# Three FFN pairs kept in PSUM through norm and convolution, the second norm's scaled input in PSUM, one square on ScalarE, and the last eight adaLN blocks later

## The chip, the core and the metric

The kernel runs on one core of a Trainium2 chip. Five engines work on their own instruction streams, each in the order in which its stream was written: TensorE (PE in the profile, its weight loads as PEld), VectorE (DVE), ScalarE (ACT), GpSimd (POOL) and SyncE (SP), which here issues the transfers. They wait for each other by semaphores. The metric is the device time of one execution in microseconds (us); lower is better.

## The reference, cut to what matters

One decoder layer on 256 tokens of width 1024 in float32. The part that the change touches is the end of the layer:

```
mod = c @ w_ada + b_ada                       # 6 x 1024 adaLN numbers
sh_m, sc_m, gt_m, sh_f, sc_f, gt_f = split(mod, 6)
h = rms_norm(x, norm_mix) * (1 + sc_m) + sh_m
...                                           # attention and delta net, mixed
x = x + gt_m * (mixed @ w_out)
h = rms_norm(x, norm_ffn) * (1 + sc_f) + sh_f
u = causal_depthwise_conv(h @ ffn_up, ffn_conv) + ffn_conv_b      # width 3
u_gate, u_val = split(u, 2)
x = x + gt_f * ((silu(u_gate) * u_val) @ ffn_down)
return rms_norm(x, norm_final)
```

FFN_DIM is 2816, that is 22 blocks of 128 channels for the gate and 22 for the value.

## The kernel before

Activations lie transposed: channels on the 128 partitions, the 256 tokens along the free axis, so that the width of 1024 is eight tiles (k = 0 to 7). Every matrix product is made from two parts of each operand: a rounded high part and the rest, the low part. For an activation these are `fh` and `fl` (`hh`/`hl`, `gh`/`gl`, `ah`/`al` elsewhere), for a weight `whi` and `wlo` (`dhi`/`dlo` for the down matrix), and one block of a product is three matmuls: high by high, low by high, high by low. `split` (L232) makes the two parts of a weight piece of 128x1024 that `rawload` (L227) has fetched: ScalarE casts the high part (L241), and GpSimd or VectorE subtracts it (L242), three pieces of eight on GpSimd at this stage. Five raw buffers turn for all such pieces, five for `whi`, four for `wlo`; the adaLN blocks use the same raw buffers (`wada`, L206 to L218: one transfer of 512 KB and one VectorE reduction, L212).

Before the FFN, the output projection (`lin` on `mxh`, L1059) gives the new residual `x1` and the sum of squares in PSUM (`ss2`). So that TensorE need not wait for the norm, the first three FFN pairs (NU = 3; a pair is the gate block and the value block of the same 128 channels) are multiplied with the un-normed input `gh`/`gl` into six PSUM banks, `up` (L1074 to L1085), with the shift as an extra column. Then `rsqrt` (L198) gives `r`; the six banks are scaled by `r` (L1092), get their shift as a bias (L1093) and are further called `u`. The normed input itself, `mt` (L1098), `fh` (L1099) and `fl` (L1100), is made for pairs 3 to 21.

For each pair f in the FFN loop (L1131): `lin` multiplies (L264, L266, L267), `fconv` (L1105) makes the three convolution taps, one on ScalarE (L1108) and two on VectorE (L1110), for the gate (`ug`) and the value (`uv`); then the gate's silu (L1144), the product with the value (L1147) and its two parts `ah` (L250) and `al` (L251). From pair 5 on, the down projection of pair f-5 follows (L1126 to L1128, into the four banks `dn`), and in pairs 4 to 11 one adaLN block of `gt_f` (L1154). The last eight pairs' down matmuls come at the end (L1163), with the residual and the last norm.

Tile's scheduler decides the order of the instructions on each engine when the kernel is built, from its own estimate of durations, and gives each PSUM tile one of eight banks. A bank is handed on as a whole: who writes the next tile into it waits for the last reader of the one before.

Of the kernel before, what the change touches and what calls it, by code (L numbers as in the profile page):

```python
# [15 lines left out]
AF = mybir.ActivationFunctionType  # L16
ALU = mybir.AluOpType
# [4 lines left out]
P = 128  # L22
D = 1024
KB = D // P
T = 256
# [8 lines left out]
NU = 3  # L34
# [9 lines left out]
PARTS = 2  # L44
OUTS = {0: 0, 1: 1, 3: 2, 5: 4, 7: 6}
QG = 1
ADA = ([0] * 4, [1] * 8, [1] * 8, 2, 4)
WARM = (2, 4)
GC = math.sqrt(2.0 / math.pi)

# [51 lines left out]
def build(tc, a, probe=None):  # L102
    nc = tc.nc
    V, S, G, TE = nc.vector, nc.scalar, nc.gpsimd, nc.tensor
    with ExitStack() as ctx:
# [8 lines left out]
        def bank(name, tag, shape=(P, 512)):  # L114
            return ps.tile(list(shape), F32, name=name, tag=tag, bufs=PB[tag])
# [7 lines left out]
        def tl(name, tag, shape=None, dt=F32):  # L123
            n, w = TAGS[tag]
            return wk.tile(list(shape or (P, w)), dt, name=name, tag=tag, bufs=n)
# [45 lines left out]
        def preload(src):  # L171

            S.activation(kcon[:, 1:2], src, AF.Abs_reciprocal_sqrt)
# [15 lines left out]
            cs = slice(512 * i, 512 * i + 512)  # L189
            TE.matmul(flat(kob[5 + i]), ones[:1], crow[:, cs], start=True, stop=True)  # L190

        def newton(y, v, t, n=1.0):

            V.tensor_tensor(t, y, y, op=ALU.mult)
            V.scalar_tensor_tensor(t, t, -0.5 / n, v, op0=ALU.mult, op1=ALU.mult)
            V.scalar_tensor_tensor(y, t, 1.5, y, op0=ALU.add, op1=ALU.mult)

        def rsqrt(v):  # L198

            r, t = tl("r", "mz"), tl("nt", "tc")  # L200
            S.activation(r, v, AF.Abs_reciprocal_sqrt, scale=1.0 / D)
            newton(r, v, t, D)
            return r


# [8 lines left out]
        def ada(n=1):  # L214

            for _ in range(n):
                m = next(mods)
                adasum(m, adaload(m))  # L218
# [34 lines left out]
        def lin(src, hh, hl, blocks=2, tag="lin"):  # L253

            parts = loadw(src)
            o = bank("lin", tag, (P, blocks, T))
            n = KB // len(parts)
            parts = [[v.rearrange("p (k c) -> p k c", k=n) for v in p] for p in parts]
            for i, (hi, lo) in enumerate(parts):
                for b in range(blocks):  # L260
                    cs = slice(b * P, b * P + P)
                    for j in range(n):
                        k = i * n + j
                        TE.matmul(o[:, b], hi[:, j, cs], hh[k], start=k == 0 and b == 0, stop=False,  # L264
                                  skip_group_check=True)
                        TE.matmul(o[:, b], hi[:, j, cs], hl[k], start=False, stop=False, skip_group_check=True)  # L266
                        TE.matmul(o[:, b], lo[:, j, cs], hh[k], start=False,  # L267
                                  stop=k == KB - 1 and b == blocks - 1, skip_group_check=True)
            return o
# [24 lines left out]
        def scaled(k):  # L294
            t = tl("mt", "tc")
            V.scalar_tensor_tensor(t, x[k], acol[:, k:k + 1], r, op0=ALU.mult, op1=ALU.mult)
            return t
# [34 lines left out]
        ac(0)  # L332
        adasum(1, wada[1])
        r = rsqrt(ssq[:, :T])
        t = scaled(0)
        shifted(0, t, V)
# [97 lines left out]
        w = wp.tile([P, D], F32, name="wraw", tag="wraw", bufs=NRAW)  # L434
        nc.sync.dma_start(out=w[:, :512], in_=a["wg"])
        w = w[:, :512].rearrange("p (k c) -> p k c", k=KB)
# [100 lines left out]
        for h in range(NH):  # L537
            for c in range(2):
                eq = bank("eq", "gd")
                u = 8 * c + h  # L540
# [12 lines left out]
                            op=ALU.add, negate=True)  # L553
# [35 lines left out]
        for p in range(4):  # L589
            o = lin(a["win"][p], hh, hl)  # L590
# [18 lines left out]
        n = range(2)  # L609
# [62 lines left out]
        def delta(p):  # L672
# [52 lines left out]
            for _ in range(3):  # L725
                newton(y_, v_, t_)
# [17 lines left out]
        def gates_z(p):  # L744
            o = lin(a["win"][14 + p], hh, hl)
            ada(ADA[0][p])
            for b in range(2):
# [243 lines left out]
        mg = [[tl(f"mg{m}{b}", "mz") for b in range(8)] for m in range(2)]  # L991
        for m in range(2):
            for p in range(4):
                o = lin(a["win"][18 + 4 * m + p], hh, hl)
                for b in range(2):
                    S.activation(mg[m][2 * p + b], o[:, b], AF.Tanh, scale=0.5)
                ada(ADA[1][4 * m + p])

# [13 lines left out]
        for p in range(4):  # L1012
            for m, (w, yh, yl) in enumerate((("pn", yah, yal), ("pg", ybh, ybl))):
                o = lin(a[w][p], yh, yl)
                ada(ADA[2][2 * p + m])
                for b in range(2):
                    t = mg[m][2 * p + b]
# [40 lines left out]
        for p in range(4):  # L1058
            o = lin(a["wo"][p], mxh, mxl)  # L1059
            ada(ADA[3])  # L1060
            residual(o, p, x1, x, gm, ss2, 4, True)
# [12 lines left out]
        ups = [[bank("up", "up" if f < 2 else "lin") for b in range(2)] for f in range(NU)]  # L1074
        for i in range(2):
            up = [[v.rearrange("p (k c) -> p k c", k=4) for v in loadw(a["up"][f][i:i + 1])[0]] for f in range(NU)]
            for j in range(4):
                k = 4 * i + j
# [7 lines left out]
        r = rsqrt(ss2[:, :T])  # L1086
        wsh = small(NU, 2)
        for f in range(NU):
            for b in range(2):
                o, u = ups[f][b], tl("u", "mg")  # L1090
                V.tensor_copy(wsh[:, f, b:b + 1], o[:, T:T + 1])
                V.tensor_tensor(u, o[:, :T], r, op=ALU.mult)  # L1092
                S.activation(u, u, AF.Identity, bias=wsh[:, f, b:b + 1])  # L1093
                ups[f][b] = u
        fh, fl = big("fh"), big("fl")
        for k in range(KB):
            t = tl("mt", "tc")
            V.scalar_tensor_tensor(t, x1[k], acol[:, 8 + k:9 + k], r, op0=ALU.mult, op1=ALU.mult)  # L1098
            S.activation(fh[k], t, AF.Identity, bias=shf[:, k:k + 1])  # L1099
            V.scalar_tensor_tensor(fl[k], t, shf[:, k:k + 1], fh[k].bitcast(F32), op0=ALU.add, op1=ALU.subtract)  # L1100
# [4 lines left out]
        def fconv(src, blk, name):  # L1105
            acc = tl(name, "mg")
            w0 = COLS["fconv"][0] + 3 * blk
            S.activation(acc, src, AF.Identity, bias=cl("fconvb", blk), scale=col[:, w0 + 2:w0 + 3])  # L1108
            for sft in (1, 2):
                V.scalar_tensor_tensor(acc[:, sft:], src[:, :T - sft], col[:, w0 + 2 - sft:w0 + 3 - sft],  # L1110
                                       acc[:, sft:], op0=ALU.mult, op1=ALU.add)
            return acc
# [18 lines left out]
        for f in range(NF):  # L1131
            if f < NU:
                o = ups[f]
            else:
                o = lin(a["up"][f], fh, fl, tag="lin" if f % 2 else "gd")
                o = [o[:, b] for b in range(2)]
            ug = fconv(o[0], f, "ug")
            uv = fconv(o[1], NF + f, "uv")

            if f >= NU:  # L1140
                t, w = o
            else:
                t, w = tl("ft", "mg"), uv
            S.activation(t, ug, AF.Silu)  # L1144
            if f == NF - 1:
                preload(t[:, :1])
            V.tensor_tensor(w, t, uv, op=ALU.mult)  # L1147
            uv = w
            acts[f] = tl("ah", "mg", dt=F32R), tl("al", "mg", dt=F32R)
            split_act(*acts[f], uv)  # L1150
            if LAG <= f < NF - TAIL:
                down(f - LAG, parts_of(f - LAG))
            if ADA[4] <= f < ADA[4] + 8:
                ada()  # L1154
# [19 lines left out]
        r = rsqrt(ss3[:, :T])  # L1174
# [70 lines left out]
```

## Time and profile before

| | |
|---|---|
| three runs | 658.63, 657.24, 657.26 us; median 657.26 |
| profiled execution | 658.84 us, of which the span from first to last instruction 657.0 us |
| busy | PE 592.5 us (90%), DVE 524.3 (80%), ACT 382.8 (58%), POOL 341.2 (52%) |
| mean granted TensorE clock | 0.954 |
| chain that ended last | PE 42%, DVE 33%, DMA 11%, issue 6%, ACT 6% |

The profile is one execution. "Idle before" an instruction is the time in which its engine stood still, with the instruction that released it behind the arrow. Busy time of an engine includes the time that an instruction, once begun, takes longer than usual. A matmul's own duration (0.28 us) overlaps the next one's, so the pace is read from counts in a stretch. The granted clock of 1.00 is 2.4 GHz, 0.50 is 1.2 GHz.

### The profile page before, as it was taken

The page shows a single profiled execution, that of the slowest core. Times are in us where ns is not written, and L with a number is a line of the kernel's source. Part 1 is how long each engine was busy: PE and PEld are TensorE (multiplying, and loading weights), DVE is VectorE, ACT ScalarE, POOL GpSimd, SP SyncE. Part 2 cuts the span into 40 slices and gives each one's busy share as a digit, 9 for nine tenths or more (in the row PEclk, how much of TensorE's full clock was granted, in tenths as well). Part 3 has the DMA queues.
Part 4 walks back from the last instruction along what each step waited for, and adds up shares of the span by engine and source line. Part 5 has one row for each costly group of instructions (what it writes and reads, how often), then busy time and mean ns, then how long its engine had stood idle before and what let it go on. Part 6 is the DMA issues. An engine that isn't in the chain of part 4 may idle for free.

```text
span 657.0 us, 13696 instructions
## 1 busy us (share of the span) xinstructions
PE 592.5 (90%) x5128; PEld 559.5 (85%) x5128; DVE 524.3 (80%) x1209; ACT 382.8 (58%) x855; POOL 341.2 (52%) x239
## 2 busy tenths in 40 slices
PE   7998997999989998999898998798967989999994
PEld 4987997988979886999777997797966979999994
DVE  5999869789998998788967779769996676675745
ACT  4335988645555676687775532565554456655443
POOL 3324996825584876475521443455552258544431
PEclk9899999899997989999999999699896989999998
DMA  7779555334784734233304557754556546553501
GB/s 287 280 278 336 217 197 193 122 129 136 228 280 169 252 131 161 66 129 130 130 33 162 175 185 256 265 210 156 193 198 252 198 166 218 193 193 129 193 1 64
DMA packets 35365, 119.73 MB, mean 182 GB/s; under 512 B 4962, under 2 KB 5730, under 8 KB 35299
## 3 DMA queue, kind: packets, MB, share of 16 engines
q1 hardware_dynamic: 35298, 118.86, 51.4%
q8 instruction: 40, 0.66, 0.4%
q14 instruction: 27, 0.21, 0.1%
HBM read 117.66 MB, written 1.18 MB: 181 GB/s over the span
## 4 chain that ended last, share of the span: by engine, by line
PE 42%; DVE 33%; DMA 11%; issue 6%; ACT 6%; SPq 1%; DVEq 0%; ACTq 0%
DMA wada<-in_ada 9%; PE lin L266 9%; PE lin L267 8%; PE lin L264 8%; DVE wada L212 7%; DVE wlo L242 4%; PE dn L1127 2%; PE dn L1128 2%; PE dn L1126 2%; DVE pp L920 2%; ACT whi L241 1%; PE y L966 1%; DVE uv L1110 1%; DVE pp L904 1%; DVE cacc L396 1%
## 5 line engine op out<-in xcount | busy, mean ns | idle before, releaser
L242 POOL TENSOR_TENSOR wlo<-wraw,whi 128x1024 fp32r<-128x1024 f32 x90 | 230.2, 2567 | 180.2 <-ACT whi L241 95.7
L241 ACT CAST whi<-wraw 128x1024 fp32r<-128x1024 f32 x144 | 150.2, 1048 | 86.1 <-PE lin L266 26.7
L264 PE MATMUL lin<-hh,whi 128*128 128x256 f32 x384 | 111.8, 291 | 1.1 <-DVE cacc L396 0.7
L267 PE MATMUL lin<-hh,wlo 128*128 128x256 f32 x384 | 111.3, 291 | 0.0
L266 PE MATMUL lin<-hl,whi 128*128 128x256 f32 x384 | 111.2, 290 | 0.0
L212 DVE CUSTOM_DVE_ANT_0 wada<-wada,cb,col 128x1024 f32<-128x1024 f32 x48 | 85.5, 1783 | 18.4 <-DMA wada<-in_ada 18.1
L266 PE MATMUL lin<-fl,whi 128*128 128x256 f32 x304 | 87.5, 289 | 2.9 <-DVE fl L1100 2.9
L264 PE MATMUL lin<-fh,whi 128*128 128x256 f32 x304 | 87.2, 288 | 0.2
L267 PE MATMUL lin<-fh,wlo 128*128 128x256 f32 x304 | 86.9, 287 | 0.0
L242 DVE TENSOR_TENSOR wlo<-wraw,whi 128x1024 fp32r<-128x1024 f32 x54 | 82.0, 1519 | 5.2 <-ACT whi L241 2.2
L264 PEld LDWEIGHTS lin<-hh,whi 128*128 128x128 f32 x384 | 74.9, 195 | 2.0 <-ACT whi L241 0.9
L267 PEld LDWEIGHTS lin<-hh,wlo 128*128 128x128 f32 x384 | 75.1, 196 | 0.6 <-issue 0.2
L266 PEld LDWEIGHTS lin<-hl,whi 128*128 128x128 f32 x384 | 75.0, 195 | 0.6
L266 PEld LDWEIGHTS lin<-fl,whi 128*128 128x128 f32 x304 | 60.3, 198 | 3.3 <-DVE fl L1100 3.3
L1126 PE MATMUL dn<-ah,dhi 128*128 128x256 f32 x176 | 49.0, 288 | 13.1 <-ACT ah L250 13.1
L264 PEld LDWEIGHTS lin<-fh,whi 128*128 128x128 f32 x304 | 60.1, 198 | 0.6 <-ACT whi L241 0.3
L267 PEld LDWEIGHTS lin<-fh,wlo 128*128 128x128 f32 x304 | 60.2, 198 | 0.0
L242 POOL TENSOR_TENSOR dlo<-wraw,dhi 128x1024 fp32r<-128x1024 f32 x14 | 34.9, 2498 | 44.0 <-ACT dhi L241 41.7
L1127 PE MATMUL dn<-al,dhi 128*128 128x256 f32 x176 | 49.3, 283 | 0.3 <-DVE al L251 0.2
L1128 PE MATMUL dn<-ah,dlo 128*128 128x256 f32 x176 | 49.0, 281 | 0.0
L1126 PEld LDWEIGHTS dn<-ah,dhi 128*128 128x128 f32 x176 | 33.6, 196 | 14.1 <-ACT ah L250 14.1
L913 ACT ACTIVATE pp<-pp,misc 128x128 f32<-128x128 f32 x64 | 28.4, 446 | 13.8 <-DVE misc L905 13.7
(410 smaller groups left out, 1620.3 us busy)
## 6 DMA issues: line engine op xcount, KB each, us to landing
wraw<-in_win SPq DMA_DIRECT2D x52, 512.0 KB, 3.7
wada<-in_ada SPq DMA_DIRECT2D x48, 512.0 KB, 4.5
wraw<-in_up SPq DMA_DIRECT2D x44, 512.0 KB, 3.8
wraw<-in_down SPq DMA_DIRECT2D x22, 512.0 KB, 3.7
wraw<-in_wko SPq DMA_DIRECT2D x16, 512.0 KB, 5.2
wraw<-in_pn SPq DMA_DIRECT2D x8, 512.0 KB, 3.5
wraw<-in_pg SPq DMA_DIRECT2D x8, 512.0 KB, 3.6
wraw<-in_wo SPq DMA_DIRECT2D x8, 512.0 KB, 4.0
```

What stands on the lines that cost most here:

```text
L212: V.tensor_tensor_reduce(w, w, cb, 1.0, cl("bada", m), ALU.mult, ALU.add, mod[:, m:m + 1])
L241: recent[S] = S.copy(hi, w).ins
L242: recent[e] = e.tensor_tensor(lo, w, hi.bitcast(F32), op=ALU.subtract).ins
L264: TE.matmul(o[:, b], hi[:, j, cs], hh[k], start=k == 0 and b == 0, stop=False, skip_group_check=True)
L266: TE.matmul(o[:, b], hi[:, j, cs], hl[k], start=False, stop=False, skip_group_check=True)
L267: TE.matmul(o[:, b], lo[:, j, cs], hh[k], start=False, stop=k == KB - 1 and b == blocks - 1, skip_group_check=True)
L396: V.scalar_tensor_tensor(acc[:, sft:], src[:, :T - sft], col[:, w0 + 3 - sft:w0 + 4 - sft], acc[:, sft:], op0=ALU.mult, op1=ALU.add)
L913: S.activation(pv, pv, AF.Exp, bias=mx[:, 1 + w, t, r:r + 1], accum_out=sm[:, 1 + w, t, r:r + 1])
L920: (G if 2 * w + t in POOLP else V).tensor_scalar(pv, pv, wt[:, 1 + w, t, r:r + 1], None, op0=ALU.mult)
L1126: TE.matmul(o, hi[:, cs], ah, start=f == 0 and b % 2 == 0, stop=False, skip_group_check=True)
L1127: TE.matmul(o, hi[:, cs], al, start=False, stop=False, skip_group_check=True)
L1128: TE.matmul(o, lo[:, cs], ah, start=False, stop=f == NF - 1 and b % 2 == 1, skip_group_check=True)
```

## The change

Four edits. ADA's last number moves the eight adaLN blocks of the FFN loop from pairs 4 to 11 to pairs 12 to 19. `rsqrt` squares its first estimate on ScalarE and not on VectorE, in all three norms (the first, the second and the last one). The six banks of the first three pairs are scaled, shifted, convolved and multiplied in place, where they were copied to SBUF by the scaling. And `mt` of the second norm lies in PSUM, two k in one bank.

```diff
-ADA = ([0] * 4, [1] * 8, [1] * 8, 2, 4)
+ADA = ([0] * 4, [1] * 8, [1] * 8, 2, 12)
...
-        def newton(y, v, t, n=1.0):
-
-            V.tensor_tensor(t, y, y, op=ALU.mult)
+        def newton(y, v, t, n=1.0, squared=False):
+
+            if not squared:
+                V.tensor_tensor(t, y, y, op=ALU.mult)
...
             S.activation(r, v, AF.Abs_reciprocal_sqrt, scale=1.0 / D)
-            newton(r, v, t, D)
+            S.activation(t, r, AF.Square)
+            newton(r, v, t, D, True)
...
-                o, u = ups[f][b], tl("u", "mg")
+                o, u = ups[f][b], ups[f][b][:, :T]
...
-            t = tl("mt", "tc")
+            if k % 2 == 0:
+                mt = bank("mt", "at", (P, 2, T))
+            t = mt[:, k % 2]
...
-            if f >= NU:
-                t, w = o
-            else:
-                t, w = tl("ft", "mg"), uv
+            t, w = o
```

The banks as the built programs have them around the second norm, in order of use:

```
bank  before                          changed
0     up (pair 2 gate), lin 5          up (pair 2 gate), lin 5
1     up (pair 2 value), dn            up (pair 2 value), dn
2     up (pair 0 gate), lin 4          up (pair 0 gate), lin 3, dn
3     up (pair 0 value), dn            up (pair 0 value), lin 4
4     up (pair 1 gate), dn             up (pair 1 gate), dn
5     lin (wo), lin 3                  lin (wo), mt k0 k1, mt k4 k5, dn
6     up (pair 1 value), dn            up (pair 1 value), lin 6
7     ss2, lin 6                       ss2, mt k2 k3, mt k6 k7
```

The order of the instructions, first on TensorE at the beginning of pair 3 (`lin_6343` before, `lin_6330` now; the numbers name buffers, a wait names the engine whose semaphore is waited for). Before:

```order
L264 MATMUL lin_6343<-fh_6234,whi_6333 128x256 [waits Activation_49]
L266 MATMUL lin_6343<-fl_6242,whi_6333 128x256 [waits DVE_49]
L267 MATMUL lin_6343<-fh_6234,wlo_6334 128x256 [waits Pool_49]
L264 MATMUL lin_6343<-fh_6235,whi_6333 128x256 [waits Activation_49]
L266 MATMUL lin_6343<-fl_6243,whi_6333 128x256 [waits DVE_49]
L267 MATMUL lin_6343<-fh_6235,wlo_6334 128x256
```

Now, at the same place, right behind the last `up` matmul:

```order
L266 MATMUL lin_6330<-fh_6228,whi_6320 128x256 [waits DVE_49,PE_49,Activation_49]
L268 MATMUL lin_6330<-fl_6236,whi_6320 128x256
L269 MATMUL lin_6330<-fh_6228,wlo_6321 128x256 [waits Pool_49]
L266 MATMUL lin_6330<-fh_6229,whi_6320 128x256 [waits Activation_49]
L268 MATMUL lin_6330<-fl_6237,whi_6320 128x256
L269 MATMUL lin_6330<-fh_6229,wlo_6321 128x256
```

The matmuls are the same; the first one's wait for VectorE is now for the first pair's product, `up_6019<-up_6018,uv_6280`, the last reader of bank 2. In the same way pair 4's first matmul waits for `al_6287` (bank 3), pair 5's for `up_6023<-up_6022,uv_6308` (bank 0), and the first down matmul for the third pair's `al` (bank 1). Down blocks stand one pair of up matmuls or so later than before: the block of pair f-5 behind pair f.

On VectorE, from the second norm on, before:

```order
L194 TENSOR_TENSOR nt_6205<-r_6204 128x256
L195 SCALAR_TENSOR_TENSOR nt_6205<-nt_6205,ss2_5692 128x256
L196 SCALAR_TENSOR_TENSOR r_6204<-nt_6205,r_6204 128x256
L1098 SCALAR_TENSOR_TENSOR mt_6250<-x10_5681,misc_69,r_6204 128x256
L1098 SCALAR_TENSOR_TENSOR mt_6254<-x11_5682,misc_69,r_6204 128x256
L1098 SCALAR_TENSOR_TENSOR mt_6258<-x12_5683,misc_69,r_6204 128x256
```

and now:

```order
L196 SCALAR_TENSOR_TENSOR nt_6205<-nt_6205,ss2_5692 128x256
L197 SCALAR_TENSOR_TENSOR r_6204<-nt_6205,r_6204 128x256
L1093 COPY misc_69<-up_6018 128x1
L1102 SCALAR_TENSOR_TENSOR mt_6244<-x10_5681,misc_69,r_6204 128x256
L1102 SCALAR_TENSOR_TENSOR mt_6251<-x12_5683,misc_69,r_6204 128x256
L1094 TENSOR_TENSOR up_6018<-up_6018,r_6204 128x256
L1104 SCALAR_TENSOR_TENSOR fl_6236<-mt_6244,misc_69,fh_6228 128x256
L1102 SCALAR_TENSOR_TENSOR mt_6244<-x11_5682,misc_69,r_6204 128x256
L1114 SCALAR_TENSOR_TENSOR ug_6276<-up_6018,col_80,ug_6276 128x255
L1104 SCALAR_TENSOR_TENSOR fl_6237<-mt_6244,misc_69,fh_6229 128x256
L1114 SCALAR_TENSOR_TENSOR ug_6276<-up_6018,col_80,ug_6276 128x254
L1104 SCALAR_TENSOR_TENSOR fl_6238<-mt_6251,misc_69,fh_6230 128x256
```

Before, all eight `mt` stood ahead of the first copy out of `up_6018`; now that copy stands ahead of the first `mt`, and `mt`, `fl` and the first pair's work are mixed.

Further on, on VectorE, the first pair's product and what stands around it, before:

```order
L1110 SCALAR_TENSOR_TENSOR uv_6290<-u_6214,col_80,uv_6290 128x255
L1110 SCALAR_TENSOR_TENSOR ug_6286<-u_6210,col_80,ug_6286 128x254
L242 TENSOR_TENSOR dlo_6562<-wraw_6559,dhi_6561 128x1024
L1110 SCALAR_TENSOR_TENSOR uv_6290<-u_6214,col_80,uv_6290 128x254
L212 ISA wada_6595,misc_69<-wada_6595,cb_95,col_80 128x1024
L212 ISA misc_69 128x1
L1147 TENSOR_TENSOR uv_6290<-ft_6294,uv_6290 128x256
L251 TENSOR_TENSOR al_6298<-uv_6290,ah_6297 128x256
```

and now:

```order
L1114 SCALAR_TENSOR_TENSOR uv_6280<-up_6019,col_80,uv_6280 128x255
L1114 SCALAR_TENSOR_TENSOR uv_6280<-up_6019,col_80,uv_6280 128x254
L1148 TENSOR_TENSOR up_6019<-up_6018,uv_6280 128x256
L244 TENSOR_TENSOR dlo_6546<-wraw_6543,dhi_6545 128x1024
L1104 SCALAR_TENSOR_TENSOR fl_6241<-mt_6258,misc_69,fh_6233 128x256
L1104 SCALAR_TENSOR_TENSOR fl_6242<-mt_6265,misc_69,fh_6234 128x256
L253 TENSOR_TENSOR al_6287<-up_6019,ah_6286 128x256
L1102 SCALAR_TENSOR_TENSOR mt_6265<-x17_5688,misc_69,r_6204 128x256
```

The product stands before the last `mt` and the last three `fl` now, 30 instructions from the copy out of `up_6018` (itself counted); no adaLN reduction (`wada`) stands between. In the changed program the eight reductions lie between the `al` of pair 7 and the `al` of pair 15, and the loads of these blocks on SP likewise behind the weights of pair 11.

## Rows read from the trace of the kernel before

**Rows 1.** The page's slices: 40 equal parts of the span, tenths.

```profile
PE   7998997999989998999898998798967989999994
```

**Rows 2.** Windows: PE, PEld, DVE, ACT, POOL busy (x instructions), clock, DMA share, GB/s.

```profile
452.00:476.00 24.00, 21.01 (x151) 20.31 (x149) 24.00 (x34) 13.29 (x20) 14.66 (x5) 0.86 0.47 167
476.00:540.00 64.00, 50.53 (x371) 48.93 (x370) 47.95 (x65) 31.31 (x49) 26.10 (x11) 0.87 0.58 209
540.00:640.00 100.00, 100.00 (x879) 100.00 (x878) 62.46 (x98) 56.85 (x90) 50.72 (x20) 1.00 0.43 153
502.50:508.00 5.50, 5.50 (x26) 5.50 (x27) 4.82 (x6) 1.41 (x2) 2.08 (x1) 0.50 0.42 144
```

**Rows 3.** Waits of PE from 452 to 540: us in total, times, longest.

```profile
PE dn L1126 <- ACT ah L250: 13.1, 5, 4.9
PE lin L266 <- DVE fl L1100: 2.9, 2, 2.5
```

**Rows 4.** Timeline of PE: start us, us, instruction, [idle before <- releaser].

```profile
450.70 0.28 PE L1085 MATMUL up<-gl,whi 128*128 128x258 f32 x1
...
452.63 0.28 PE L264 MATMUL lin<-fh,whi 128*128 128x256 f32 x1
...
493.38 0.79 PE L1126 MATMUL dn<-ah,dhi 128*128 128x256 f32 x2 [4.89 <-ACT ah L250]
...
502.45 1.23 PE L1126 MATMUL dn<-ah,dhi 128*128 128x256 f32 x4 [3.58 <-ACT ah L250]
```

**Rows 5.** Timeline of DVE, second norm and first pairs.

```profile
445.65 2.61 DVE L194 TENSOR_TENSOR nt<-r 128x256 f32<-128x256 f32 x1
...
449.22 3.26 DVE L1098 SCALAR_TENSOR_TENSOR mt<-x,misc,r 128x256 f32<-128x256 f32 x8
...
455.18 5.49 DVE L1100 SCALAR_TENSOR_TENSOR fl<-mt,misc,fh 128x256 fp32r<-128x256 f32 x3
...
462.12 0.47 DVE L1100 SCALAR_TENSOR_TENSOR fl<-mt,misc,fh 128x256 fp32r<-128x256 f32 x1
...
462.92 0.14 DVE L1091 COPY misc<-up 128x1 f32<-128x1 f32 x1
462.98 0.41 DVE L1092 TENSOR_TENSOR u<-up,r 128x256 f32<-128x256 f32 x1
...
467.95 2.61 DVE L1110 SCALAR_TENSOR_TENSOR uv<-u,col,uv 128x254 f32<-128x254 f32 x1
...
473.83 2.60 DVE L1147 TENSOR_TENSOR uv<-ft,uv 128x256 f32<-128x256 f32 x1
...
501.20 0.43 DVE L1147 TENSOR_TENSOR lin<-lin,uv 128x256 f32<-128x256 f32 x1 [0.51 <-ACT lin L1144]
...
507.18 1.21 DVE L242 TENSOR_TENSOR wlo<-wraw,whi 128x1024 fp32r<-128x1024 f32 x1
```

**Rows 6.** Timeline of POOL in the same stretch.

```profile
442.25 5.73 POOL L242 TENSOR_TENSOR wlo<-wraw,whi 128x1024 fp32r<-128x1024 f32 x2 [1.89 <-PE up L1085]
...
454.89 5.10 POOL L242 TENSOR_TENSOR wlo<-wraw,whi 128x1024 fp32r<-128x1024 f32 x2 [6.91 <-ACT whi L241]
```

**Rows 7.** Timeline of ACT at the second norm.

```profile
444.44 1.04 ACT L241 CAST whi<-wraw 128x1024 fp32r<-128x1024 f32 x1
...
449.74 2.51 ACT L1099 ACTIVATE fh<-mt,misc 128x256 fp32r<-128x256 f32 x6 [4.26 <-DVE mt L1098]
```

**Rows 8.** Groups of DVE from 476 to 540: busy, mean ns, idle before, releaser.

```profile
L212 DVE CUSTOM_DVE_ANT_0 wada<-wada,cb,col 128x1024 f32<-128x1024 f32 x6 | 11.9, 1977 | 5.4 <-DMA wada<-in_ada 5.4
```

**Rows 9.** Timeline of DVE: first and last `al` of 14 after 540.

```profile
547.92 0.42 DVE L251 TENSOR_TENSOR al<-lin,ah 128x256 fp32r<-128x256 f32 x1 [0.44 <-ACT ah L250]
...
633.37 0.42 DVE L251 TENSOR_TENSOR al<-lin,ah 128x256 fp32r<-128x256 f32 x1 [0.78 <-ACT ah L250]
```

**Rows 10.** Timeline of DVE, the squares of the first and the last norm.

```profile
12.47 0.42 DVE L194 TENSOR_TENSOR nt<-r 128x256 f32<-128x256 f32 x1
...
648.94 0.42 DVE L194 TENSOR_TENSOR nt<-r 128x256 f32<-128x256 f32 x1 [2.13 <-ACT r L201]
```

## The prediction

> **What bounds the kernel now.** First the slices of the page: TensorE is at nine tenths almost throughout, but in slices 30 and 31 (476 to 509) its digits fall to 6 and 7 [rows 1]. Then the sums by stage: I split at 452, where the FFN pairs 3 to 21 begin, and at 540. From 540 to 640 TensorE is busy all the time at clock 1.00, with 879 matmuls in 100 us, 0.114 us each. From 452 to 476 and from 476 to 540 it has 151 and 371 matmuls in 24 and 64 us [rows 2]. At 0.114 they would need 17.2 and 42.2 us: 6.8 and 21.8 us are lost, 28.6 in all. That is what a change here can win or add to. Who ends TensorE's waits there: 2.9 us `fl` from VectorE, 13.1 us `ah` from ScalarE, five times [rows 3]. The rest of the 28.6 us is mostly the half clock after a stop: from 502.5 to 508.0 the granted clock is 0.50 (1.2 GHz of 2.4) and 26 matmuls take 5.5 us, 0.21 us each [rows 2], after a stop of 3.58 us [rows 4].
>
> Why `ah` is late: VectorE. From 452 to 476 it is busy 24.00 of 24 us [rows 2], but by waiting. A `fl` takes 0.47 us alone, three take 5.49; a product of the early pairs takes 2.60 us where one with an operand in PSUM takes 0.43; a convolution tap takes 2.61 [rows 5]. At 445 and 455 GpSimd was in splits of weights [rows 6] (and in the other slow cases too), and both VectorE operands lay in SBUF. One such wait costs 2.61 - 0.47 = 2.14 us.
>
> The Trainium skill, "SBUF — State Buffer", section "SBUF: two separate sides", says that VectorE instructions with two SBUF inputs and GpSimd share a port pair, held for a whole instruction. The trace agrees (2.61 against 0.47 us); by the rule every such instruction that is left can still wait.
>
> **The change part by part.**
>
> *Squares on ScalarE.* Three VectorE squares go, three ScalarE squares come. In the second norm VectorE's square took 2.61 us behind GpSimd [rows 5]. Now ScalarE squares after its cast that ends at 445.48, about 0.42 us (2.51/6) [rows 7]; `nt`, with an operand in PSUM, ends near 446.4. The next, `r`, has both in SBUF and waits for GpSimd until 447.98 [rows 6]: 448.4 instead of 449.2. That 0.8 us is worth nothing, since the next VectorE row is now the copy out of `up_6018`, which waits for TensorE's last matmul on that bank, 450.70 + 0.28 = 451.0 [rows 4]. In the last norm 0.42 us on one engine replaces 0.42 on the other, both in line: 0, within 0.1 either way [rows 10]. In the first the square leaves VectorE's line (0.42 [rows 10]) and lies beside ScalarE's wait for its first weights; VectorE's work behind it waits for weights too, so I count 0, at best 0.4.
>
> *`mt` and `u` in PSUM.* `fl` now has one SBUF operand, as have the taps and products of the first three pairs: they no longer wait for GpSimd. The price is in the banks. Banks 0 to 4 and 6 hold the six halves, 5 and 7 hold `mt`: none is left for pair 3. Its first matmul, at 452.63 before [rows 4], now waits until the first pair's product has read `up_6018`; pair 4 waits for that pair's `al`, pair 5 for the third pair's product. So TensorE stands still from 452.6 until VectorE has done the 30 instructions from that copy through the product: 6 copies at 0.06 from start to start, 7 `mt` at 0.41, 6 scalings at 0.41, 5 `fl` at 0.47, 4 taps at 0.47, one `wlo` at 1.21 and the product at 0.43 [rows 5], 11.6 us, thus 462.6 at the earliest (the others' durations overlap a little, which pays for the short waits for ScalarE). Of the 30, the `mt` and the `wlo` still have two SBUF operands, and GpSimd has three splits in this stretch (two of pair 4, one of a down block) whose turn comes then. Each can hold VectorE 2.14 us: between 462.6 and 469.0. I take one and a half, 465.8: at 455 both splits of GpSimd's row of two held a `fl` [rows 5, 6], but a VectorE row may also come first. TensorE's stop is then 13.2 us (10.0 to 16.4). After it I count 26 matmuls at 0.21 instead of 0.114 us [rows 2], 2.5 us more. Pair 3's later `fl` come while TensorE is in its first half at that rate. New loss: 15.7 us.
>
> *The adaLN blocks of pairs 4 to 11 go to 12 to 19.* From 476 to 540 six of them kept VectorE busy 11.9 us and made it wait 5.4 us for their loads [rows 8], (11.9 + 5.4)/6 = 2.9 us each. Their loads also leave SP's queue and the five raw buffers in front of pairs 5 to 12, so weights are asked for earlier. Without them VectorE makes a pair in (633.37 - 547.92)/13 = 6.57 us [rows 9], while TensorE needs 72 x 0.114 = 8.2. So I let the 21.8 us of stops from 476 to 540 go; next late is TensorE itself. The first three `ah` are there long before their down blocks, whose order is five pairs behind the up matmuls. What comes back: in pairs 12 to 19 VectorE needs 6.57 + 2.9 = 9.5 us against 8.2, 1.3 too many eight times, 10 us behind at the end. Behind a waiting adaLN block stand the taps and the `wlo` of coming pairs. But four banks turn for the up matmuls, so a pair waits for the `al` four before it: some three pairs, 24 us, of slack cover it. Bounds: 0, and one stop as the longest here (4.89 [rows 4]) with its half clock, 7.4. I take 2.5, near the lower, because the three pairs hold more than 10. SP and the transfers have room: 0.43 of the DMA engines from 540 to 640 [rows 2].
>
> **The sum.** Lost before 28.6, after 15.7 + 2.5 = 18.2: 10.4 us won. The profiled execution took 658.84 (span 657.0 and 1.84 around it), so 648.4; it is 1.58 above the median of the runs, 657.26, and against that 646.9.
>
> **Rivals.**
> 1. *GpSimd stays out of the way.* Pair 3 starts at 462.6, the rest as above: 3.2 us better, 643.7. For it: a VectorE row that comes first is not held, and only 8 of the 30 can be. Against it: the two long waits at 455 [rows 5].
> 2. *All three splits are met, and a stop comes back with the adaLN blocks.* 469.0 and 7.4: 3.2 + 4.9 worse, 655.0. For it: VectorE at 9.5 us a pair.
> 3. *The stops are only moved* (slower). The banks held cost 15.7, and the adaLN blocks bring pairs 12 to 19 what they brought pairs 4 to 11: the whole 21.8 us come again. 28.6 - 15.7 - 21.8 = -8.9: 666.2. It decides once the later stops exceed 12.9 us. For it: VectorE was the late one there [rows 3, 8]. Against it: from 540 on the pairs have a settled rhythm, with VectorE busy 62 of 100 us [rows 2], and nothing else crowds in.
> 4. *The change does not hold TensorE up*: pair 3 starts at 452.6 with its half-clock time as before; then 28.6 less about 4 is won, 632.7. The waits as built speak against it.
>
> The Trainium skill, "PSUM — Partial Sum Buffer", section "Summary: rules for kernel authors", says to empty PSUM promptly because it is tight. This speaks against the change: by it alone the holding costs and gives nothing back, which is rival 3. The rows of before cannot show which side wins.
>
> **Chances and range.** The forecast 0.58; rival 1 0.15; rival 2 0.11; rival 3 0.10; rival 4 0.02; the early loss and the later gain about equal 0.04. Two executions of this kernel can be told apart from about 0.2%, 1.3 us, on. Faster 0.86, same 0.04, slower 0.10. The range runs from rival 1 without any stop left (643.7 - 2.5 = 641.2) to rival 2: 641 to 655.
>
> **What would show it.** Right: a stop of TensorE of 10 to 16 us before the first `lin` on `fh`, ended by the product `up`, half clock behind it; `fl` at 0.5 us; no wait of `dn` for `ah` over 1 us before 530; adaLN blocks between roughly 540 and 610 with TensorE still at nine tenths. Wrong: `dn` waits for `ah` again, or `lin` for `al` or `wlo`, in the second half of the pairs; or a first stop that a transfer or a weight ends.

## The result, and the profile after

The changed kernel takes 653.24 us (median of 16 runs, 651.31 to 657.27), the kernel before 658.55 (16 runs): 0.9927 of its time, 95% interval 0.9911 to 0.9944. It is faster by 0.73%, some 4.8 us (the two medians differ by 5.3), where 10.4 were forecast. The profiled execution after took 651.43 us (span 649.4), 7.4 less than the profiled one before; it is among the fastest of its 16, and the run e6_tail below shows one place where 2 us can come or go.

The stages after, to be held against [rows 2] (columns as there):

```profile
452.00:476.00 24.00, 15.21 (x109) 15.03 (x109) 20.71 (x43) 17.92 (x32) 13.56 (x5) 0.79 0.45 154
476.00:540.00 64.00, 64.00 (x563) 64.00 (x563) 41.19 (x61) 35.36 (x55) 36.63 (x14) 1.00 0.62 210
540.00:640.00 100.00, 93.64 (x790) 91.43 (x789) 65.41 (x100) 51.71 (x88) 42.40 (x16) 1.00 0.45 156
```

From 452 to 476 there are 109 matmuls: 24 - 109 x 0.114 = 11.6 us lost (6.8 before). From 476 to 540 TensorE is never idle, 563 matmuls where there were 371: the 21.8 us are gone. But from 540 on it is no longer full. Who ends TensorE's waits from 440 to 640 (total, times, longest), beside [rows 3]:

```profile
PE lin L266 <- DVE up L1148: 8.8, 1, 8.8
PE lin L269 <- DVE wlo L244: 3.9, 5, 1.4
PE lin L269 <- POOL wlo L244: 1.8, 1, 1.8
PE dn L1132 <- POOL dlo L244: 0.6, 2, 0.4
```

The first line is the hold that the prediction describes: pair 3 waits for the first pair's product. The next two are new: `lin` waits for low parts of weights (the split's subtraction, L242 before, is L244 now), which no row of before shows. VectorE's timeline around one of these stops, and then TensorE's:

```profile
566.01 0.42 DVE L253 TENSOR_TENSOR al<-lin,ah 128x256 fp32r<-128x256 f32 x1 [1.59 <-ACT ah L252]
566.35 2.93 DVE L244 TENSOR_TENSOR wlo<-wraw,whi 128x1024 fp32r<-128x1024 f32 x1
569.21 0.99 DVE L1114 SCALAR_TENSOR_TENSOR ug<-lin,col,ug 128x255 f32<-128x255 f32 x2
570.83 0.48 DVE L1114 SCALAR_TENSOR_TENSOR uv<-lin,col,uv 128x255 f32<-128x255 f32 x1 [0.63 <-ACT uv L1112]
572.84 2.13 DVE L214 CUSTOM_DVE_ANT_0 wada<-wada,cb,col 128x1024 f32<-128x1024 f32 x1 [1.53 <-DMA wada<-in_ada]
```

```profile
568.48 0.28 PE L268 MATMUL lin<-fl,whi 128*128 128x256 f32 x1
569.34 0.39 PE L269 MATMUL lin<-fh,wlo 128*128 128x256 f32 x1 [0.58 <-DVE wlo L244]
```

The low part ends at 566.35 + 2.93 = 569.28, and the matmul that reads it starts at 569.34, 0.86 us after the one in front of it: 0.75 lost, of which the list names 0.58. VectorE's groups from 476 to 640 (busy, mean ns | idle before) show what stands in the low parts' way:

```profile
L244 DVE TENSOR_TENSOR wlo<-wraw,whi 128x1024 fp32r<-128x1024 f32 x14 | 24.5, 1747 | 0.3 <-PE lin L269 0.3
L214 DVE CUSTOM_DVE_ANT_0 wada<-wada,cb,col 128x1024 f32<-128x1024 f32 x8 | 17.6, 2194 | 9.3 <-DMA wada<-in_ada 9.3
```

The eight adaLN blocks hold VectorE 17.6 us at work (waits for GpSimd included) and 9.3 us standing still for their loads, 26.9 in all, 3.4 a block; [rows 8] gave 2.9.

### The profile page after: what moved, and what is told of

The parts are those of the page before. It is cut to its first block, busy times and chain, and to the rows that moved or that the text cites. A ratio compares the mean times of both kernels' runs of the same rounds, so it can differ in the third digit from the quotient of the medians.

```text
span 649.4 us, 13709 instructions
## 1 busy us (share of the span) xinstructions
PE 583.3 (90%) x5128; PEld 550.4 (85%) x5128; DVE 512.1 (79%) x1206; ACT 381.5 (59%) x858; POOL 342.1 (53%) x239
## 4 chain that ended last, share of the span: by engine, by line
PE 40%; DVE 35%; DMA 10%; ACT 7%; issue 6%; POOL 1%; SPq 0%; DVEq 0%; ACTq 0%; POOLq 0%
PE lin L266 8%; PE lin L268 8%; PE lin L269 8%; DMA wada<-in_ada 8%; DVE wlo L244 7%; DVE wada L214 6%; DVE pp L922 2%; PE dn L1132 2%; PE dn L1131 2%; PE dn L1130 2%; PE y L968 1%; ACT whi L243 1%; DVE cacc L398 1%; DMA wraw<-in_down 1%; DVE tb L577 1%
## 5 line engine op out<-in xcount | busy, mean ns | idle before, releaser
L244 POOL TENSOR_TENSOR wlo<-wraw,whi 128x1024 fp32r<-128x1024 f32 x90 | 228.8, 2551 | 165.3 <-ACT whi L243 97.4
L266 PE MATMUL lin<-fh,whi 128*128 128x256 f32 x304 | 85.6, 282 | 8.8 <-DVE up L1148 8.8
L244 DVE TENSOR_TENSOR wlo<-wraw,whi 128x1024 fp32r<-128x1024 f32 x54 | 88.1, 1632 | 2.8 <-ACT whi L243 2.2
L268 PE MATMUL lin<-fl,whi 128*128 128x256 f32 x304 | 85.5, 281 | 0.0
L266 PEld LDWEIGHTS lin<-fh,whi 128*128 128x128 f32 x304 | 58.3, 192 | 9.0 <-ACT fh L1103 9.0
L269 PEld LDWEIGHTS lin<-fh,wlo 128*128 128x128 f32 x304 | 58.3, 192 | 7.0 <-DVE wlo L244 5.0
L244 POOL TENSOR_TENSOR dlo<-wraw,dhi 128x1024 fp32r<-128x1024 f32 x14 | 37.4, 2676 | 49.8 <-ACT dhi L243 48.4
L268 PEld LDWEIGHTS lin<-fl,whi 128*128 128x128 f32 x304 | 58.4, 192 | 0.0
L1132 PEld LDWEIGHTS dn<-ah,dlo 128*128 128x128 f32 x176 | 33.1, 188 | 1.0 <-POOL dlo L244 1.0
```

Of the source, the lines that this page charges most:

```text
L244: recent[e] = e.tensor_tensor(lo, w, hi.bitcast(F32), op=ALU.subtract).ins
L269: TE.matmul(o[:, b], lo[:, j, cs], hh[k], start=False, stop=k == KB - 1 and b == blocks - 1, skip_group_check=True)
L1132: TE.matmul(o, lo[:, cs], ah, start=False, stop=f == NF - 1 and b % 2 == 1, skip_group_check=True)
```

## The experiments

Ratios are to the kernel before, on the same chip, with 95% intervals. 0.001 is 0.66 us.

**Each edit alone, and the blocks away.** e1_move_alone is the kernel before with `ADA = (..., 12)` and nothing else. e2_not_moved and e3_no_blocks start from the changed kernel:

```diff
 e2_not_moved
-ADA = ([0] * 4, [1] * 8, [1] * 8, 2, 12)
+ADA = ([0] * 4, [1] * 8, [1] * 8, 2, 4)
 e3_no_blocks
-            if ADA[4] <= f < ADA[4] + 8:
-                ada()
...
-        V.tensor_copy(gm[:, 8:], mod[:, 40:48])
+        V.tensor_copy(gm[:, 8:], mod[:, 32:40])
```

> The kernel before, with nothing but the adaLN blocks moved to pairs 12 to 19. Theory A (the blocks make both the stops of 476 to 540 before and the loss of some 10 us after 540 now): the 21.8 us go, 6.8 us of 452 to 476 stay, some 10 us come after 540, so 11 to 12 us better than before, near 646; TensorE full from 476 to 540. Theory B (the PSUM edits took the stops of 476 to 540 away, by sparing VectorE the waits for GpSimd): most of the 21.8 us stay and 10 us come on top, 656 to 668.

> The changed kernel with the adaLN blocks back in pairs 4 to 11. Theory A: the loss of 452 to 476 (11.6 us) stays, the 21.8 us of 476 to 540 come back, nothing is lost after 540: 33.4 us lost against 28.6, so 4 to 6 us slower than before, near 662. Theory B: only 11.6 us are lost, 17 us better than before, near 641.

> The changed kernel without the last eight adaLN blocks (no load, no reduction; the gate of the last residual takes other adaLN numbers, so the output is not the reference's). Theory A: only the 11.6 us of 452 to 476 are lost, 10 us less than in the changed kernel: near 643, and TensorE goes from 470 to the residual without a stop over 0.3 us. Theory B (the loss after 540 is the share of the splits between VectorE and GpSimd, and the down blocks' order, with or without the blocks): within 2 us of the changed kernel, stops for `wlo` after 560 as now.

Measured: e1 652.74 us, 0.9909 [0.9880, 0.9938]; e2 655.52, 0.9957 [0.9936, 0.9978]; e3 643.68, 0.9768 [0.9741, 0.9794]. e3 settles the loss after 540: without the blocks the changed kernel is 9.6 us faster by the medians and 10.5 by the ratios, as theory A said. In its trace the one wait of TensorE left from 440 to 640 is the hold:

```profile
PE lin L266 <- DVE up L1148: 8.8, 1, 8.8
```

and from 540 to 620 it does 704 matmuls; the changed kernel (second fence) does 637, 7.6 us fewer:

```profile
540.00:620.00 80.00, 80.00 (x704) 80.00 (x704) 45.90 (x73) 43.67 (x69) 39.34 (x16) 1.00 0.45 152
```

```profile
540.00:620.00 80.00, 74.27 (x637) 72.99 (x636) 55.44 (x81) 38.88 (x63) 36.65 (x14) 1.00 0.56 195
```

For e1 and e2 both theories missed. Moving the blocks gains 6 us alone and the PSUM edits gain 3 alone, but together they gain 5, not 9. Each run has one large stop of its own: e1 6.55 us at 566 (`lin` for `al`), e2 8.07 at 526 (`lin` for `al` too) beside a hold of 11.95. On top of the move, the PSUM edits and the square gain nothing that the intervals show (e1 against the changed kernel).

**`mt` out of PSUM.** To free banks 5 and 7:

```diff
-            if k % 2 == 0:
-                mt = bank("mt", "at", (P, 2, T))
-            t = mt[:, k % 2]
+            t = tl("mt", "tc")
```

> The changed kernel with `mt` in SBUF again, so that banks 5 and 7 are free for pairs 3 and 4; the first three pairs stay in PSUM. Theory A (the stop of 8.8 us is the banks): it goes with its half clock, at most 3 us of waits for `fl` come, 6 to 10 us better than the changed kernel, 643 to 647. Rival (the stop is VectorE's work in front of `fl` and only takes another name): a stop of 6 us or more before the first `lin`, ended by `fl` or `fh`, and within 2 us of the changed kernel.

Measured: 659.72 us, 1.0006 [0.9989, 1.0024], neither theory's number. The hold is gone (waits of 3.3 us for `fl`, 2.5 and later 6.5 for `al` in its place), but something unasked came with it: its matmuls stand farther apart at the full clock. From 600 to 635, first e4, then e1, TensorE busy without a break in both:

```profile
600.00:635.00 35.00, 35.00 (x297) 35.00 (x297) 23.47 (x34) 20.07 (x32) 17.93 (x7) 1.00 0.28 99
```

```profile
600.00:635.00 35.00, 35.00 (x311) 35.00 (x311) 21.73 (x32) 18.58 (x31) 16.11 (x6) 1.00 0.27 92
```

297 matmuls against 311. Start to start it is 0.1186 us in e4 in most stages, from the first on; the other kernels have 0.113 to 0.118 before the FFN and 0.114 in most of it. So its time can't be set against theirs as it is. At its own pace TensorE loses 19.4 us between the last `up` matmul and the last `dn` matmul (190.2 us less 1440 x 0.1186), the changed kernel 20.7 (184.9 less 1440 x 0.114). By this estimate the stop only made room for others, nearer to the rival than to theory A; but a slower TensorE also leaves VectorE more time, so this is not shown. e12 puts most tiles at other addresses (NMISC = 1488 for 1280).

> `mt` in SBUF as in the run e4_mt_sbuf, with 832 bytes of unused SBUF in front, so that `hh` and most of the activations lie at other addresses (161600 and 169792 leave the same rest by 8192, 168960 does not). In that run matmuls stood 0.1186 us apart at the full clock from the first stage on, against 0.113 to 0.118 in the others. If the addresses are the cause: 0.114 us in the FFN, and 646 to 651. If it is something else in that program: 0.1186 again and 658 to 661.

Measured: 657.77 us, 0.9994 [0.9975, 1.0013], again 0.118 to 0.119. This other place of the tiles did not change the pace; what sets it stays open, and with it what the banks alone cost.

**What of a block costs.** e7 reduces 8 of 1024 columns, e10 reduces a tile that needs no load, in the same place, e11 asks for each load two pairs earlier (the edits are cut to their main lines):

```diff
 e7_short
+            n = 8 if m >= 40 else D
-            V.tensor_tensor_reduce(w, w, cb, 1.0, ...)
+            V.tensor_tensor_reduce(w[:, :n], w[:, :n], cb[:, :n], 1.0, ...)
 e10_pinned
-                ada()
+                m = next(mods)
+                with tc.issue_after(recent[V]):
+                    V.tensor_tensor_reduce(junk, cb, cb, 1.0, ...)
 e11_raw_ahead
-            if ADA[4] <= f < ADA[4] + 8:
-                ada()
+            if ADA[4] - 2 <= f < ADA[4] + 6:
+                with tc.issue_after(recent[nc.sync]):
+                    held.append(adaload(next(mods)))
+            if ADA[4] <= f < ADA[4] + 8:
+                with tc.issue_after(recent[V]):
+                    adasum(28 + f, held.pop(0))
```

> The changed kernel with the last eight reductions over 8 of 1024 columns (the gate of the last residual is then not the reference's): loads, raw buffers and waits for the loads stay, VectorE's own time of some 2 us each goes. If VectorE's time is what costs: 643 to 646. If it is the waiting for the loads, in order on VectorE (10.5 us in all after 476): 650 to 653.

> The changed kernel with the last eight reductions over a tile that has been in SBUF all along (no load; the gate of the last residual is not the reference's): VectorE's own time stays, the loads, their raw buffers and the waits for them go. If VectorE's time is what costs: 650 to 653. If it is the waiting for the loads or the raw buffers: 643 to 646.

> The changed kernel with the last eight reductions over a tile that has been in SBUF all along, each queued on VectorE behind the split of its pair, so that they stay in pairs 12 to 19 (no load; the gate of the last residual is not the reference's). Theory V (VectorE's own time, some 2 us a block with its waits for GpSimd, is the price): 650 to 653, `lin` waiting for `wlo` after 560. Theory L (the loads are the price: they pass SP's queue and the five raw buffers, and VectorE stands still for them in order): 642 to 645, no stop over 0.5 us after 470.

> The changed kernel with each of the last eight loads asked for two pairs ahead of its reduction (same raw buffers, same places of the reductions). Theory L1 (VectorE's standing still for a load, 9.3 us in all, is the price): the waits for `wada` fall below 3 us and the time to 645 to 648. Theory L2 (the raw buffers are the price: a buffer that holds an adaLN block is missing for weights, and here it is held two pairs longer): 653 to 658, `lin` waiting for `wlo` as now or more.

e8 is e10 without the `issue_after`: 660.98 us, 1.0044. It answers another question: the scheduler put the eight reductions, which wait for nothing, at 224 to 257 us, and the first `lin` of the FFN started at 482.56 instead of 461.48. e7 took 657.34, 0.9991 [0.9968, 1.0014]; e10 651.55, 0.9879 [0.9858, 0.9900]; e11 653.60, 0.9917 [0.9894, 0.9941]. Their blocks on VectorE from 476 to 640, in this order:

```profile
L215 DVE CUSTOM_DVE_ANT_0 wada<-wada,cb,col 128x8 f32<-128x8 f32 x8 | 10.3, 1285 | 14.4 <-DMA wada<-in_ada 14.4
```

```profile
L1158 DVE CUSTOM_DVE_ANT_0 junk<-cb,col 128x1024 f32<-128x1024 f32 x8 | 18.9, 2360 | 0.0
```

```profile
L214 DVE CUSTOM_DVE_ANT_0 wada<-wada,cb,col 128x1024 f32<-128x1024 f32 x8 | 16.6, 2087 | 0.0
```

Against e3 the blocks cost (0.9927 - 0.9768) x 658.5 = 10.5 us in the changed kernel, 7.3 in e10, 9.8 in e11, 14.7 in e7. VectorE's time for them (its waits for GpSimd included), without any load, is thus the larger part (theory V of e10). Taking the work away does not help while the loads stay (e7; both its theories missed): VectorE comes to the load earlier and stands there, and a reduction of 8 columns takes 0.23 us at its shortest but 1.29 on average. So VectorE is held 24.7 us instead of 26.9. Asking earlier takes its standing still to 0.0 and gains nothing (e11, theory L2). Its trace fits L2's reason, weights that come late in turn: `lin` waits 1.2 us for `whi`, a row that the changed kernel does not have. Why e7 is 4 us worse than the changed kernel is not settled.

**Other places.** e5 has `f in (6, 8, ..., 20)`. The others put some blocks behind the down blocks at the end, where TensorE has matmuls in hand (e6 as an example; e15: pairs 8, 12, 16 and five late; e17: pairs 11, 15 and six late; e18: all late). e13, e14 and e16 are the kernel before with the places of e3, e6 and e15.

```diff
 e6_tail
-            if ADA[4] <= f < ADA[4] + 8:
+            if f in (12, 15, 18, 21):
                 ada()
...
         for f in range(NF - LAG - TAIL, NF - 2):
             down(f, parts_of(f))
+            if f >= NF - 6:
+                ada()
```

> The changed kernel with the eight adaLN blocks behind every second pair, 6 to 20. Theory A1 (the loss after 540 is crowding: VectorE at 9.5 us a pair against TensorE's 8.2, eight pairs in a row): one block in two pairs makes 8.0 us, the loss goes, 643 to 646. Theory A2 (each block costs about 1.2 us by itself, wherever it stands, since `wlo` or `al` stands behind it on VectorE): 651 to 654 as the changed kernel.

> The changed kernel with four adaLN blocks behind pairs 12, 15, 18 and 21 and four behind the down blocks of pairs 16 to 19 at the end, where TensorE has 20 us of matmuls in hand and VectorE little to do. Theory A1: 643 to 646. Theory A2: half the cost is left, 647 to 649. Rival: the late loads push the last residual back, 650 or more, with TensorE's last matmuls over and a wait of the residual for `wada` or the adaLN numbers.

> The kernel before without the last eight adaLN blocks (no load, no reduction; the gate of the last residual takes other adaLN numbers). It asks what the PSUM edits are worth when the blocks are out of the way; with them it was 643.7 (e3_no_blocks). Theory P (the PSUM edits cost their hold of 11.6 us and spare nothing else): only the 6.8 us of 452 to 476 are lost, 637 to 641. Theory Q (they spare VectorE waits for GpSimd that stop TensorE even without the blocks): stops for `ah` or `al` between 476 and 520 stay, 645 to 651.

> The kernel before with four adaLN blocks behind pairs 12, 15, 18 and 21 and four behind the down blocks of pairs 16 to 19 (the places of e6_tail, which gave 649.0 with the PSUM edits). Theory P: 643 to 647. Theory Q: 650 to 655.

> The changed kernel with three adaLN blocks behind pairs 8, 12 and 16 and five behind the down blocks of pairs 15 to 19. If a block costs nothing while `wlo` stands 8 us or more ahead of its use, and four pairs lie between two blocks to win the lead back: 643 to 647, better than e6_tail by 2 to 5. If the five late ones hold up the low parts of the last weights: 649 to 653.

> The kernel before with the adaLN blocks at the places of e15_tail5. Theory P: 638 to 644, the best of all. Theory Q: 647 to 653, worse than e15_tail5.

> The changed kernel with two adaLN blocks behind pairs 11 and 15 and six behind the down blocks of pairs 14 to 19. By the lead of `wlo` (10 us at pair 11, won back within four pairs) neither of the two costs anything, and no stop is left between 470 and 620: 644 to 647. If six late blocks hold up the low parts of the last weights or the last residual: 648 to 653.

> The changed kernel with all eight adaLN blocks behind the down blocks of pairs 14 to 19 (two behind each of the first two). The time of the kernel without the blocks was 643.7. If VectorE's idle time there takes all eight: 643 to 646. If the eight loads (4 MB, at some 230 GB/s 18 us) and the down weights behind them on SP come late: 649 to 656, `dn` waiting for `dhi` or `dlo`, or the residual for the adaLN numbers.

Measured: e5 651.04 us (A2), e6 649.02 (the upper end of A2), e13 643.47, e14 649.63, e15 648.25 and e16 655.64 (none of their theories), e17 648.16 and e18 651.48 (the second of each). The places, without the PSUM edits and the square, and with them (ratio, interval):

```
adaLN blocks                     without                        with
pairs 4 to 11                    1 (before)                     0.9957 [0.9936, 0.9978]  e2
pairs 12 to 19                   0.9909 [0.9880, 0.9938]  e1    0.9927 [0.9911, 0.9944]  (changed)
none                             0.9780 [0.9754, 0.9805]  e13   0.9768 [0.9741, 0.9794]  e3
12, 15, 18, 21, four late        0.9865 [0.9839, 0.9890]  e14   0.9853 [0.9828, 0.9879]  e6
8, 12, 16, five late             0.9964 [0.9944, 0.9984]  e16   0.9848 [0.9815, 0.9882]  e15
every second of 6 to 20                                         0.9891 [0.9863, 0.9919]  e5
11, 15, six late                                                0.9825 [0.9799, 0.9852]  e17
all late                                                        0.9895 [0.9870, 0.9920]  e18
```

Across the rows: with no block, or blocks from pair 12 on, the two columns do not differ beyond their intervals. Only where blocks stand in pairs 4 to 11 do the PSUM edits win, 2.8 us in the first row and 7.6 in the fifth. Theories P and Q of e13 both failed: e13 stands at 643.47 us and e3 at 643.68. The waits of e13 from 440 to 640 say why, beside the single line of e3:

```profile
PE dn L1126 <- ACT ah L250: 4.0, 2, 2.0
PE lin L266 <- DVE fl L1100: 2.0, 2, 1.6
PE dn L1127 <- DVE al L251: 1.6, 1, 1.6
```

```profile
452.00:476.00 24.00, 20.42 (x171) 19.81 (x170) 22.48 (x33) 17.07 (x25) 17.32 (x6) 1.00 0.59 192
476.00:540.00 64.00, 59.97 (x489) 59.31 (x488) 40.59 (x65) 37.40 (x59) 32.01 (x13) 0.95 0.57 184
```

4.5 us are lost in the first stretch and 8.3 in the second, 12.8 in all, in many small waits; with the edits it is 11.2 (112 matmuls in e3) and 0, in one hold. The edits gather the early loss into one stop and hardly make it smaller.

Down the right column: two to four blocks in the pairs and the rest late beat eight in pairs 12 to 19, and all late is worse again than two. e17 has 0.9825 against 0.9927 of the changed kernel, the lowest of those that compute everything. Its interval meets those of e6 and e15, which also beat the changed kernel, so the order of these three is not shown. e17 loses little in the pairs and some at the end, where its loads meet the last down weights:

```profile
PE lin L266 <- DVE up L1148: 8.8, 1, 8.8
PE dn L1130 <- ACT dhi L243: 1.5, 1, 1.5
PE dn L1130 <- ACT ah L252: 1.1, 1, 1.1
PE lin L269 <- DVE wlo L244: 0.8, 2, 0.4
PE dn L1132 <- DVE dlo L244: 0.8, 1, 0.8
```

e15's one late stop (3.41 us at 502.74, `lin` for `al`) and e5's (3.23 at 503.88) suggest that a block behind pair 6 or 8 is early even with the PSUM edits: e17, whose first block is behind pair 11, has no stop there.

## Why the prediction was wrong

*What bounds the kernel*: right. VectorE was late from 452 to 540, and the change left no stop from 476 to 540, with `fl` at 0.47 us and no `dn` wait for `ah`, as said. But the prediction put this down to the blocks alone, and that was too much: with only the blocks moved, e1 still loses 64 - 494 x 0.114 = 7.7 us there. (The share of GpSimd in the splits is three of five pieces at this stage, 22 of the 38 low parts from pair 3 on, and not three of eight as the description of the kernel has it; no term rests on it.)

*The banks held, 15.7 us*: the mechanism was right, the size was 11.6, and the stop of 8.79 us lies below the 10 to 16 of the sign. VectorE's work was counted well: 30 instructions, 11.6 us and one wait for GpSimd. But it began at 448.09, not at 451.0:

```profile
446.19 1.98 DVE L197 SCALAR_TENSOR_TENSOR r<-nt,r 128x256 f32<-128x256 f32 x1
448.09 0.15 DVE L1093 COPY misc<-up 128x1 f32<-128x1 f32 x1
...
452.56 1.22 DVE L244 TENSOR_TENSOR wlo<-wraw,whi 128x1024 fp32r<-128x1024 f32 x1
...
453.83 2.45 DVE L1102 SCALAR_TENSOR_TENSOR mt<-x,misc,r 128x256 f32<-128x256 f32 x1
...
460.90 0.43 DVE L1148 TENSOR_TENSOR up<-up,uv 128x256 f32<-128x256 f32 x1
```

I had taken the copy to wait for the matmul at 450.70. It did not: it followed `r` with no idle time, 4.3 us before the last `up` matmul started (452.41). 448.09 + 11.6 and one wait of 2.0 (the `mt` at 453.83) give 461.7; TensorE starts at 461.48, after 8.79 us, with 0.79 as the mean clock of the stretch.

How many splits VectorE meets varies by itself. In e6 the order up to here is the same, the hold is 10.92, and the difference is one row, VectorE's and then GpSimd's:

```profile
452.80 3.37 DVE L244 TENSOR_TENSOR wlo<-wraw,whi 128x1024 fp32r<-128x1024 f32 x1
```

```profile
452.74 2.34 POOL L244 TENSOR_TENSOR wlo<-wraw,whi 128x1024 fp32r<-128x1024 f32 x1 [4.62 <-ACT whi L243]
```

Here GpSimd is not held and VectorE is, 3.37 - 1.22 = 2.15 us. In the changed kernel's profile VectorE is not held (1.22 above), and GpSimd's two splits beside it are long:

```profile
452.50 5.98 POOL L244 TENSOR_TENSOR wlo<-wraw,whi 128x1024 fp32r<-128x1024 f32 x2 [4.62 <-ACT whi L243]
```

In both GpSimd's row starts 0.06 us earlier. The Trainium skill ("SBUF — State Buffer", "SBUF: two separate sides") says that whoever starts first holds the port pair for a whole instruction. The traces agree that one of the two is held, in 2 us steps; which one, these starts do not tell. That is the forecast's step of 2.14. It may be part of why the median won less than the profiled execution; the other executions have no trace, so that is not shown.

*The adaLN blocks in pairs 12 to 19, 2.5 us (0 to 7.4)*: this step failed. They cost 10.5 us by the ratios of the changed kernel and e3, and 9.2 in the two traces. I had worked out that VectorE would be 10 us behind at the end, and set against it three pairs, 24 us, that the banks of the up matmuls would cover. But `lin` needs the low parts of its weights too, and VectorE makes them on the same stream, behind the blocks. Matching each low part in VectorE's order with the matmul that reads it first, its lead over TensorE in the changed kernel is 10.4 us at pair 10, 9.5 at pair 12, 6.2 at 13, 2.1 at 15 and 0.1 or less from 16 on; in e3 it stays between 7.8 and 12.4 from pair 12 to 19. Two rows of e3, VectorE's low part for pair 16 and its first reader, are the counterpart of the stop at 569 above:

```profile
558.02 1.98 DVE L244 TENSOR_TENSOR wlo<-wraw,whi 128x1024 fp32r<-128x1024 f32 x1
```

```profile
567.80 0.28 PE L269 MATMUL lin<-fh,wlo 128*128 128x256 f32 x1
```

So the cover was 10 us and not 24. That alone does not make 9.2 us: at the 1.3 us a block of the prediction, 10 us would have lasted for all eight. It lasted for five, the ones on VectorE from 517.90 to 560.91. In e3 the lead falls by 2.4 us over the same pairs (10.2 at pair 10, 7.8 at pair 16), so each block took 1.6, and the pairs themselves the rest.

Nor does the lead come back in time. After the last block (585.44 to 588.02) three more stops follow:

```profile
602.51 0.38 PE L269 MATMUL lin<-fh,wlo 128*128 128x256 f32 x1 [0.84 <-DVE wlo L244]
607.31 0.38 PE L269 MATMUL lin<-fh,wlo 128*128 128x256 f32 x1 [1.79 <-POOL wlo L244]
611.72 0.39 PE L269 MATMUL lin<-fh,wlo 128*128 128x256 f32 x1 [1.36 <-DVE wlo L244]
```

The traces of e3 and e17 say why. The last three pairs have no down block, and TensorE takes 5.5 us for one (in e3 pair 20 starts at 594.9, pair 21 at 600.4), not the 8.2 that the prediction counts up to pair 19. There low parts are used faster than they are made: even without blocks, in e3, the lead falls from 12.4 at pair 19 to 7.8 at 20 and 2.8 at 21. The changed kernel comes to these pairs with none. Of the 9.2 us by which it falls behind e3, 2.9 are lost up to the start of pair 19 (592.9) and 5.0 in pairs 19 to 21, behind the last block. A lead can be won back where pairs have down blocks: in e17 it is 0.1 us at pair 15 and 6.8 at pair 19, with no block between. I had named "`lin` for `wlo`, in the second half" as a sign of being wrong, and that is what came.

Low parts are not always what runs out first: in e1 the same eight blocks end in the 6.55 us for `al`, the wait that the prediction did count, while low parts lead by 11.

*The sum*, over the 1440 matmuls from the last `up` to the last `dn` (193.1 us before, 184.9 after and 175.7 in e3, less 1440 x 0.114): 28.9 lost before, 20.7 after, of which 11.5 are the hold with its half clock (e3) and 9.2 the blocks. The stage won 8.2, the profiled executions differ by 7.4, and 10.4 were forecast. The two misses partly cancel, 4 us too much for the hold and 7 too little for the blocks: that the forecast is not farther off is luck. *One more assumption fell without touching it*: that the move gains 21.8 and the PSUM edits lose 8.9, each by itself. e1 and e2 say 6 and a gain of 3. Of the 21.8 us, 7.7 are left from 476 to 540 in e1 and 64 - 476 x 0.114 = 9.7 in e2: either edit alone took more than half.

*The squares*: no row contradicts the 0 (`nt` takes 0.42 at 445.73 and `r` waits for GpSimd, as described); they were not tried alone.

*The rivals*: rival 1's start of pair 3, 462.6, came about (461.48), but not by its reason: one split was met, and VectorE began 2.9 us earlier. Rival 3's place was right (stops come back with the blocks), with 9.2 us below its 12.9, so that the change does not get slower. Rival 2's time, 655.0, is nearest to the median, but by other numbers: one split met in this trace and not three, and six short stops for `wlo` instead of one long. On the rule of the Trainium skill that PSUM is to be emptied promptly ("PSUM — Partial Sum Buffer", "Summary: rules for kernel authors"): the trace agrees that holding costs, a stop of 8.8 to 12 us in every run that keeps `mt` and the six banks in PSUM. Against it, e13 beside e3 shows that it gives as much back here.

## What to carry to other kernels

Slack is as long as the shortest thing that runs ahead: before work is moved onto an engine, follow every operand that the bound engine takes from it (in the changed kernel low parts, 10 us ahead) and not only the buffer that looks deepest (banks, 24 us). Ask too where the bound engine gets faster and uses the slack up by itself (here the last three pairs). Two edits that cure the same stop do not add up; try each alone and with the cause away before adding their gains. Work with no deadline belongs where the engine that waits for it has its operands already, spread until its loads meet others.

## What the runs showed of the hardware that was not expected

Matmuls of one shape at a granted clock of 1.00 do not have one pace: 0.113 to 0.114 us start to start in most of the FFN, stretches of 0.118 elsewhere (the stage at 72 to 88 us has 0.1133 in the kernel before and 0.1178 in the changed one, with the same matmuls), and 0.118 to 0.119 in most stages of e4 and e12. In the 35 us shown that is 14 matmuls in 311, 4.5%. Neither the granted clock nor the transfers tell it (DMA share 0.00 at 620 to 635 in e4, the same pace), and one other place of the tiles (e12) did not change it. So a kernel can be slower for a reason that none of its rows names; before two kernels' times are compared, their pace in a stretch where TensorE is never idle is worth a look.
